# Recurrence gates written into the decay buffer, one more raw weight buffer, and the new instruction order that goes with it

## The chip, the core and the metric

The kernel runs on one core of a Trainium2 chip. The metric is the device time of one execution in microseconds (us). Five engines work side by side, each with its own queue of instructions that it takes strictly in order: PE (TensorE, the matmuls), DVE (VectorE), ACT (ScalarE), POOL (GpSimd) and SP (SyncE, which here issues the loads). An instruction that waits holds up all that stands behind it on its engine.

## The reference: what is computed

A sequence of 256 tokens of width 1024 goes through one recurrent layer (RG-LRU), then keys and values are made once, then comes one attention layer, then a last normalisation. All is fp32. The part that the change touches is the recurrent mixer:

```
h = rmsnorm(x) * (1 + scale(c)) + shift(c)
u, g = split(h @ w_in)
u = causal_conv4(u)
r  = sigmoid(block_diag(u, w_a) + b_a)
gi = sigmoid(block_diag(u, w_x) + b_x)
log_a = -8 * r * softplus(-lam)
a    = exp(log_a)
b_in = sqrt(-expm1(2 * log_a)) * (gi * u)
hs   = scan(a, b_in)                 # h[t] = a[t] * h[t-1] + b_in[t]
x1   = x + gate(c) * ((hs * silu(g)) @ w_out)
```

After it, `x1` is normalised and modulated again (by columns called `colsmk` below), and `k, v = split(h @ w_kv)`; with one block of 256 keys the attention is plain causal attention.

## The kernel before

**Order.** The program records every operation in a `Plan` and then simulates it with a table of costs (`_forward`, `order`). Which ready operation an engine takes next is decided by an urgency per operation, and that urgency is shaken by the list of random seeds `KEEP`. The result is one fixed order for each engine, which is issued as it stands (`issue`). So another seed list, or another set of buffers, gives another order everywhere, though the operations stay the same. All instructions come out of one recorder and carry its line: L434, or L187 for those that the planner may give either to ACT or to DVE (`copy`, `affine`, `scale`). They are told apart by the names of their tiles.

**Weights.** 132 blocks of up to 512 KB come through SP's queue into `NRAW` raw buffers (`rawp`). Each block of a large product is split into a high and a low part (`split_into`: a CAST that makes `..._hi`, then a subtraction on DVE that makes `..._lo`, both 128x1024), and the product is three matmuls (`mm3`). Blocks of the modulation (`g`, `mkh`, `mkc`) feed groups of four small matmuls into `gvg` and `gvmk`, or are summed on DVE and ACT (`maccg`, `macmkh`, `macmkc`) first.

**The recurrent layer.** `conv` makes `uc` on DVE. The rest runs in two halves `j` = 0, 1 of 512 channels, each in two groups of 256 channels. For a group, PE makes `pa` and `px` (block-diagonal products with `uc`); ACT makes the sigmoid of `pa` into `rr`, and `tx`, the tanh form of the second gate, from `px`. For a half, ACT then makes tanh of `rr` into `qg`, exp of `rr` into `ag` (the decays), and a square root of `qg` in place. `ag` and `qg` are the two halves of the tile `aq`. The tables of ACT for sigmoid and tanh, for exp and for the square root differ, so that each switch is an ACT_TABLE_LOAD. DVE then makes `wgx`, runs four scans over `aq`, and multiplies by `sg` (the silu path); `y_hi` (a cast) and `y_lo` (on DVE) follow for each quarter of the channels. The tile `rr` has one buffer, and both halves use it.

**Behind it.** `out_rows("wo")` multiplies by `w_out`: PE takes the four tiles kt 0 to 3 (first half of the channels) for all outputs, 48 matmuls with `r_wo` as target, then some `gvmk` groups, then kt 4 to 7 piece by piece, again 48, then the remaining `gvmk` groups. kt 0, 1 need the first `y_hi`, kt 2, 3 the second, and kt 4 to 7 the third and fourth. `mod_gate("g0")` makes `gsg` from `gvg`; POOL moves it into a row and spreads it over all partitions as `gate_g` (PARTITION_BROADCAST). `resid` then makes each of the four pieces of `x1` (name `x`) with a multiplication by `gate_g` and an addition of `xr` on DVE. `rms` takes four squares (`sq_b`, ACT), two roots (`rv_b`, ACT) and short operations on DVE (`rb_b`, `rn_b`, `ry_b`, `rt_b`), once for each 128 tokens. `norm_T` scales (`xn_b`) and transposes on PE (`tp_b`, eight for each 128 tokens), `x1T` is copied back, `hrmk` applies `colsmk`, `hk_hi` and `hk_lo` are its parts, and the product `v` begins with the first `hk_hi`. From there on PE works through `v`, `k`, `q`, `g`, the attention and `r_wp`.

Of the kernel before, what the change touches and what calls it, by code (L numbers as in the profile page):

```python
# [10 lines left out]
F32 = mybir.dt.float32  # L11
# [3 lines left out]
AF = mybir.ActivationFunctionType  # L15
# [8 lines left out]
NH = 8  # L24
EPS = 1e-6
NEG = -1e30
NRAW = 12
NSPL = 4
NWARM = 20
NWARM2 = 4  # L30
# [9 lines left out]
    g1-1  # L40
"""
KEEP = (
    174134411, 1363847499, 501561012, 479182050, 55063396, 1262196190, 1895791361, 70921978,
    2025245939, 522247948, 1081885112, 902321754, 1806762868, 318745555, 812710329,
    423182004, 2012214809, 1111379318, 858955501, 119445705, 1610912521, 1462030052,
    1370424399,
)

MK_DVE = (2, 3)
# [404 lines left out]
def kernel(ctx: ExitStack, tc: tile.TileContext, x, mod_b, final_norm_g, vecs, pack, out):  # L454
# [5 lines left out]
    V, A, PE, G, SP = (plan.engine(e) for e in ("vector", "scalar", "tensor", "gpsimd", "sync"))  # L460
# [399 lines left out]
    baT = pbT[:, 40:48]  # L860
# [29 lines left out]
    p4 = const.tile([P, KT], F32, name="p4")  # L890
    n8 = const.tile([P, KT], F32, name="n8")
# [34 lines left out]
    for j in range(2):  # L926
# [171 lines left out]
    scale = 1.0 / math.sqrt(P)  # L1098
# [110 lines left out]
```

## Time and profile before

| | |
|---|---|
| median of 3 runs | 255.78 us (255.24 to 255.79) |
| the profiled execution | 255.34 us |
| its span in the trace | 253.6 us, 4919 instructions |
| TensorE clock granted, mean | 0.994 of full speed |
| PE busy | 241.7 us (95%) |
| DVE busy | 210.0 us (83%) |
| ACT busy | 160.0 us (63%) |
| POOL busy | 17.3 us (7%) |
| ACT table loads | 13, 1283 ns each |

The sum of the prediction is made against the profiled execution: 255.34 us, that is a span of 253.6 us and 1.7 us around it. In the timeline views a line gives the start, the length, the engine, the operation with the tile that it writes and those that it reads, and a count where several follow each other; a bracket at the end is the idle time of the engine ahead of it and what ended it.

### The profile page before, as it was taken

The numbers are of one execution on the slowest core, as the hardware profiler recorded it, in microseconds if no ns is written. First come the engines' busy times: TensorE is split into PE (matmuls) and PEld (weight loads), VectorE is DVE, ScalarE is ACT, GpSimd is POOL, SyncE is SP. The second block draws the span as 40 slices with busy tenths as digits, with TensorE's granted clock in tenths as the row PEclk, the third lists the DMA queues.
The fourth block names the chain that finished last, engine by engine and source line by source line (L and its number), as shares of the span: only waits on it lengthen the run. The fifth ranks groups of instructions, "written<-read, shape, count | busy, mean of one in ns | idle before, by whom it ended". The sixth has DMA issues, their size and how long they took to land.

```text
span 253.6 us, 4919 instructions
## 1 busy us (share of the span) xinstructions
PE 241.7 (95%) x1862; PEld 216.0 (85%) x1862; DVE 210.0 (83%) x383; ACT 160.0 (63%) x288; POOL 17.3 (7%) x24
## 2 busy tenths in 40 slices
PE   8899999999999999989999999999999999999980
PEld 8789899998888777857898898999999998879870
DVE  4577399899999999999979998998446999697583
ACT  6675563697599995389834374784438374894252
POOL 4000000000000036200000000010000000023220
PEclk9999999999999999999999999999999999999997
DMA  6999999996599957999999999989965400000003
GB/s 237 410 409 405 408 408 408 410 406 249 149 361 412 378 197 283 405 410 410 406 409 390 400 412 406 406 301 381 388 216 183 169 3 0 1 3 1 1 10 156
DMA packets 20359, 72.24 MB, mean 285 GB/s; under 512 B 2536, under 2 KB 2800, under 8 KB 20336
## 3 DMA queue, kind: packets, MB, share of 16 engines
q1 hardware_dynamic: 19728, 71.20, 72.3%
q0 software_dynamic: 464, 0.54, 0.8%
q8 instruction: 14, 0.23, 0.4%
q10 hardware_dynamic: 144, 0.20, 0.2%
q14 instruction: 9, 0.07, 0.1%
HBM read 70.87 MB, written 1.05 MB: 284 GB/s over the span
## 4 chain that ended last, share of the span: by engine, by line
PE 66%; DVE 19%; ACT 8%; issue 3%; DMA 1%; SPq 0%; DVEq 0%; ACTq 0%
PE g L434 9%; PE v L434 9%; PE u L434 9%; PE r_wp L434 8%; PE pj_wkb L434 5%; PE pj_wqb L434 5%; PE k L434 5%; PE q L434 4%; DVE uc L434 4%; PE ga L434 3%; DVE x L434 3%; PE sc L434 3%; PE oT L434 2%; DVE wo_lo L434 2%; DVE sg L434 2%
## 5 line engine op out<-in xcount | busy, mean ns | idle before, releaser
L434 PE MATMUL g<-h_hi,wgb_lo 128*128 128x256 f32 x64 | 18.0, 282 | 0.0
L434 PE MATMUL g<-h_hi,wgb_hi 128*128 128x256 f32 x64 | 18.0, 281 | 0.0
L434 PE MATMUL g<-h_lo,wgb_hi 128*128 128x256 f32 x64 | 18.0, 281 | 0.0
L434 PE MATMUL u<-h_hi,wu_hi 128*128 128x256 f32 x64 | 17.0, 289 | 0.6 <-ACT h_hi L434 0.6
L434 ACT ACT_TABLE_LOAD x13 | 16.7, 1283 | 0.9 <-PEq L1191 0.7
L434 PE MATMUL u<-h_hi,wu_lo 128*128 128x256 f32 x64 | 17.2, 287 | 0.0
L434 PE MATMUL u<-h_lo,wu_hi 128*128 128x256 f32 x64 | 17.0, 283 | 0.0
L434 DVE SCALAR_TENSOR_TENSOR maccg<-g,csT,maccg 128x1024 f32<-128x1024 f32 x12 | 15.4, 1283 | 0.2
L434 PE MATMUL r_wp<-wp_hi,o_hi 128*128 128x512 f32 (+1 forms) x40 | 14.3, 357 | 0.0
L434 PE MATMUL r_wp<-wp_lo,o_hi 128*128 128x512 f32 (+1 forms) x40 | 14.2, 356 | 0.0
L434 PE MATMUL r_wp<-wp_hi,o_lo 128*128 128x512 f32 (+1 forms) x40 | 14.1, 358 | 0.0
L434 POOL DMA_DIRECT2D row_g<-gsg x8 | 4.2, 532 | 143.2 <-DVE gsg L434 84.8
L434 PE MATMUL v<-wv_hi,hk_hi 128*128 128x512 f32 x32 | 12.4, 397 | 0.6 <-ACT hk_hi L187 0.6
L434 PE MATMUL r_wo<-wo_hi,y_hi 128*128 128x512 f32 x32 | 12.5, 401 | 0.3 <-ACT y_hi L187 0.3
L434 PEld LDWEIGHTS u<-h_hi,wu_hi 128*128 128x128 f32 x64 | 11.4, 189 | 1.6 <-ACT h_hi L434 0.8
L434 DVE TENSOR_TENSOR wgb_lo<-wgb,wgb_hi 128x1024 fp32r<-128x1024 f32 x8 | 9.7, 1218 | 3.7 <-ACT wgb_hi L187 3.7
L434 PE MATMUL v<-wv_lo,hk_hi 128*128 128x512 f32 x32 | 12.6, 395 | 0.0
L434 PE MATMUL r_wo<-wo_lo,y_hi 128*128 128x512 f32 x32 | 12.5, 395 | 0.0
L434 PE MATMUL v<-wv_hi,hk_lo 128*128 128x512 f32 x32 | 12.5, 395 | 0.0
L187 ACT CAST wgb_hi<-wgb 128x1024 fp32r<-128x1024 f32 x8 | 8.4, 1050 | 6.4 <-PE g L434 3.6
L434 PE MATMUL r_wo<-wo_hi,y_lo 128*128 128x512 f32 x32 | 12.1, 394 | 0.0
L434 PEld LDWEIGHTS g<-h_hi,wgb_hi 128*128 128x128 f32 x64 | 12.1, 188 | 0.0
(300 smaller groups left out, 865.4 us busy)
## 6 DMA issues: line engine op xcount, KB each, us to landing
g<-in_pack_dram SPq DMA_DIRECT2D x16, 512.0 KB, 5.9
wu<-in_pack_dram SPq DMA_DIRECT2D x8, 512.0 KB, 10.3
wo<-in_pack_dram SPq DMA_DIRECT2D x8, 512.0 KB, 6.2
mkh<-in_pack_dram SPq DMA_DIRECT2D x8, 512.0 KB, 6.8
mkc<-in_pack_dram SPq DMA_DIRECT2D x8, 512.0 KB, 7.1
wv<-in_pack_dram SPq DMA_DIRECT2D x8, 512.0 KB, 9.9
m1h<-in_pack_dram SPq DMA_DIRECT2D x8, 512.0 KB, 8.6
m1c<-in_pack_dram SPq DMA_DIRECT2D x8, 512.0 KB, 8.5
```

Source lines behind the costliest of these rows:

```text
L187: self.record(eng, fn, args, kw, lambda f=f, args=args, kw=kw: f(*args, **kw))
L434: self.plan.record(self.name, fn, args, kw, lambda: f(*args, **kw))
```

## The change

Three things. The tile `rr` is gone: the sigmoid goes into `ag`, tanh reads `ag`, and exp works in place on `ag`. The 4 KB for each partition that this frees hold a 13th raw buffer. And the seed list is new, 36 seeds in place of 23, so that the whole order is another one.

```diff
-NRAW = 12
+NRAW = 13
...
 KEEP = (
-    174134411, 1363847499, 501561012, 479182050, 55063396, 1262196190, 1895791361, 70921978,
...
+    235379739, 161345772, 1729185277, 1372182491, 1720230322, 837705437, 372798370,
...
         ag, qg = aq[:, 0:4], aq[:, 4:8]
-        rr = tmp.tile([P, 4, S], F32, tag="rr", name=f"rr{j}", bufs=1)
...
-                A.activation(rr[:, 2 * h + m], pr[:, m * S:(m + 1) * S], AF.Sigmoid, bias=baT[:, dd])
+                A.activation(ag[:, 2 * h + m], pr[:, m * S:(m + 1) * S], AF.Sigmoid, bias=baT[:, dd])
...
-            A.activation(qg[:, m], rr[:, m], AF.Tanh, scale=p4[:, dd])
+            A.activation(qg[:, m], ag[:, m], AF.Tanh, scale=p4[:, dd])
...
-            A.activation(ag[:, m], rr[:, m], AF.Exp, scale=n8[:, dd])
+            A.activation(ag[:, m], ag[:, m], AF.Exp, scale=n8[:, dd])
```

The number of matmuls and of table loads stays as it is (1621 and 13), and the orders of POOL and SP are the same; the recorder's lines are L436 and L189 in the new kernel. On PE the products follow each other as before with small exchanges. In the gate products `pa` and `px` now alternate group by group: four matmuls `pa`, four `px`, the next group's four `pa` and four `px`. Of the `gvmk` groups one now stands behind the `gvg` groups ahead of the first `r_wo`, three stand between kt 0, 1 and kt 2, 3 of `r_wo`, and two between kt 2, 3 and kt 4; before, all six stood in that last place. Two groups `gvm` that interrupted `pj_wkb` in two places now stand together. In the other places that count:

ACT before, from the last gates of the second half (`rr_344`, `aq_343`) to its square root; the two `y_hi` are those of kt 0, 1 and kt 2, 3:

```order
L187 CAST y_hi<-sg_323 128x512
L187 CAST wo_1_hi<-wo_1_129 128x1024
L434 ACTIVATE tx_350<-px_349,hbx 128x256
L434 ACTIVATE aq_343<-rr_344,p_301 128x256 x4
L187 CAST y_hi<-sg_323 128x512
L434 ACT_TABLE_LOAD
L434 ACTIVATE aq_343<-rr_344,n_302 128x256 x4
L434 ACTIVATE tg_pj_wgc_351_356<-pj_wgc_351 128x512
L434 ACT_TABLE_LOAD
L434 ACTIVATE aq_343<-aq_343 128x1024
L187 CAST wo_3_hi<-wo_3_135 128x1024
```

ACT now, the same place:

```order
L189 CAST wo_1_hi<-wo_1_129 128x1024
L189 CAST y_hi<-sg_323 128x512
L436 ACTIVATE aq_342<-aq_342,p_301 128x256
L436 ACTIVATE tx_345<-px_344,hbx 128x256
L436 ACTIVATE aq_342<-aq_342,p_301 128x256 x3
L436 ACT_TABLE_LOAD
L436 ACTIVATE aq_342<-aq_342,n_302 128x256 x2
L436 ACTIVATE tg_pj_wgc_349_354<-pj_wgc_349 128x512
L436 ACTIVATE aq_342<-aq_342,n_302 128x256 x2
L436 ACT_TABLE_LOAD
L436 ACTIVATE aq_342<-aq_342 128x1024
L189 CAST y_hi<-sg_323 128x512
```

The second `y_hi` has moved from ahead of the exps of the second half to behind its square root: two table loads, four exps, one tanh and the square root now stand ahead of it. In the first half the square root now comes ahead of the exps, and four casts of `wo` stand between the first half's gates and the first `y_hi`, where two stood.

DVE before, from the first product with `sg` of the second half to the first multiplications of `resid` (`x_357`):

```order
L434 TENSOR_TENSOR sg_323<-aq_343,sg_323 128x512
L434 TENSOR_TENSOR wo_3_lo<-wo_3_135,wo_3_hi 128x1024
L434 SCALAR_TENSOR_TENSOR aq_343<-aq_343,wgx 128x256
L434 TENSOR_TENSOR y_lo<-sg_323,y_hi 128x512
L434 TENSOR_TENSOR sg_323<-aq_343,sg_323 128x512
L434 TENSOR_TENSOR wo_2_lo<-wo_2_136,wo_2_hi 128x1024
L434 TENSOR_TENSOR y_lo<-sg_323,y_hi 128x512
L434 TENSOR_TENSOR wo_3_lo<-wo_3_137,wo_3_hi 128x1024
L434 SCALAR_TENSOR_TENSOR macmkh<-mkh_140,csT,macmkh 128x1024
L434 SCALAR_TENSOR_TENSOR macmkc<-mkc_141,csT,macmkc 128x1024
L434 TENSOR_TENSOR x_357<-r_wo_361,gate_g_377 128x512
L434 TENSOR_TENSOR x_357<-r_wo_362,gate_g_377 128x512
```

DVE now, from the cast of the third `y_hi` to the first multiplication of `resid` (`x_355`):

```order
L189 CAST y_hi<-sg_323 128x512
L436 TENSOR_TENSOR y_lo<-sg_323,y_hi 128x512
L436 TENSOR_TENSOR wo_3_lo<-wo_3_135,wo_3_hi 128x1024
L436 TENSOR_TENSOR wo_2_lo<-wo_2_134,wo_2_hi 128x1024
L436 TENSOR_TENSOR wo_3_lo<-wo_3_137,wo_3_hi 128x1024
L436 SCALAR_TENSOR_TENSOR aq_342<-aq_342,wgx 128x256
L436 TENSOR_TENSOR wo_2_lo<-wo_2_136,wo_2_hi 128x1024
L436 TENSOR_TENSOR sg_323<-aq_342,sg_323 128x512
L436 SCALAR_TENSOR_TENSOR macmkc<-mkc_141,csT,macmkc 128x1024
L436 TENSOR_TENSOR y_lo<-sg_323,y_hi 128x512
L436 SCALAR_TENSOR_TENSOR macmkh<-mkh_140,csT,macmkh 128x1024
L436 TENSOR_TENSOR wv_lo<-wv_146,wv_hi 128x1024
```

Between the second half's multiplication into `wgx` and the first `x` there are now five subtractions of a low part (four `wo`, one `wv`) where three stood, three `y_lo` where two stood, and a cast of `y_hi` that ACT made before. The three `wgx` and scan instructions ahead of the piece shown are the same in both.

DVE before, from the last addition of `resid` to the scaling `xn_b` of the first 128 tokens (the names `ry_b_396` and `ry_b_408` are the first and second 128 tokens):

```order
L434 TENSOR_TENSOR x_357<-x_357,xr 128x512
L434 TENSOR_SCALAR rb_b_403<-ss_b_402,eps 128x1
L434 SCALAR_TENSOR_TENSOR rt_b_397<-ry_b_396,rn_b_395 128x1
L434 TENSOR_SCALAR rb_b_403<-ss_b_402,neps 128x1
L434 SCALAR_TENSOR_TENSOR ry_b_396<-rt_b_397,ry_b_396 128x1
L187 TENSOR_SCALAR xn_b_398<-x_357,ry_b_396 128x1024
```

DVE now, from the same addition to the scaling of the second 128 tokens (`ry_b_394` the first, `ry_b_406` the second 128 tokens):

```order
L436 TENSOR_SCALAR rn_b_393<-ss_b_391,rb_b_389 128x1
L189 CAST wv_hi<-wv_152 128x1024
L436 TENSOR_SCALAR rn_b_405<-ss_b_403,rb_b_401 128x1
L436 RECIPROCAL ry_b_394<-rv_b_392 128x1
L436 SCALAR_TENSOR_TENSOR rt_b_395<-ry_b_394,rn_b_393 128x1
L436 RECIPROCAL ry_b_406<-rv_b_404 128x1
L436 SCALAR_TENSOR_TENSOR rt_b_407<-ry_b_406,rn_b_405 128x1
L436 SCALAR_TENSOR_TENSOR ry_b_394<-rt_b_395,ry_b_394 128x1
L189 TENSOR_SCALAR xn_b_396<-x_355,ry_b_394 128x1024
L436 STREAM_TRANSPOSE gTmk<-gvmk 128x512
L436 SCALAR_TENSOR_TENSOR ry_b_406<-rt_b_407,ry_b_406 128x1
L189 TENSOR_SCALAR xn_b_408<-x_355,ry_b_406 128x1024
```

Before, the first 128 tokens were finished while the last piece of `x` was still being made, and the second `xn_b` was ACT's. Now the chains of both run interleaved behind the last addition, on ACT all four squares stand ahead of both roots, and both `xn_b` are DVE's.

## Rows read from the trace of the kernel before

**Rows 1.** Waits of PE, longest after the start: us in total, times, longest.

```profile
PE tp_b L434 <- ACT x1T L187: 0.8, 1, 0.8
```

**Rows 2.** Timeline of PE, the gate products.

```profile
61.06 0.60 PE L434 MATMUL pa<-uc,gax 128*128 128x256 f32 x2
...
64.54 1.89 PE L434 MATMUL pa<-uc,gax 128*128 128x256 f32 x8
66.27 1.46 PE L434 MATMUL px<-uc,gax 128*128 128x256 f32 x6
```

**Rows 3.** Timeline of ACT, both halves' gates, up to the second half's square root.

```profile
66.47 0.84 ACT L434 ACTIVATE rr<-pa,vT 128x256 f32<-128x256 f32 x2 [3.09 <-PE pa L434]
...
70.66 0.46 ACT L434 ACTIVATE tx<-px,hbx 128x256 f32<-128x256 f32 x1
...
77.82 1.57 ACT L434 ACTIVATE rr<-pa,vT 128x256 f32<-128x256 f32 x4
...
82.74 1.10 ACT L187 CAST wo_hi<-wo 128x1024 fp32r<-128x1024 f32 x1
83.69 0.53 ACT L434 ACTIVATE tx<-px,hbx 128x256 f32<-128x256 f32 x1
...
85.65 0.65 ACT L187 CAST y_hi<-sg 128x512 fp32r<-128x512 f32 x1
86.32 1.28 ACT L434 ACT_TABLE_LOAD   x1
...
92.09 1.03 ACT L187 CAST wo_hi<-wo 128x1024 fp32r<-128x1024 f32 x1
```

**Rows 4.** Timeline of PE, both halves of `r_wo` and the `gvmk` runs.

```profile
82.94 0.50 PE L434 MATMUL r_wo<-wo_hi,y_hi 128*128 128x512 f32 x1 [0.32 <-ACT y_hi L187]
...
94.32 0.64 PE L434 MATMUL gvmk<-mkh,csB 128*32 128x256 f32 x8
...
96.50 0.61 PE L434 MATMUL gvmk<-mkc,csB 128*32 128x256 f32 x8
97.05 0.50 PE L434 MATMUL r_wo<-wo_hi,y_hi 128*128 128x512 f32 x1
...
108.41 0.64 PE L434 MATMUL gvmk<-macmkh,ones 128*32 128x256 f32 x8
```

**Rows 5.** Timeline of DVE, from the second half's `wgx` to the first `xn_b`.

```profile
92.26 1.23 DVE L434 TENSOR_TENSOR wgx<-aq,wgx 128x1024 f32<-128x1024 f32 x1
...
95.29 0.67 DVE L434 TENSOR_TENSOR sg<-aq,sg 128x512 f32<-128x512 f32 x1
95.88 1.22 DVE L434 TENSOR_TENSOR wo_lo<-wo,wo_hi 128x1024 fp32r<-128x1024 f32 x1
97.01 0.69 DVE L434 TENSOR_TENSOR_SCAN aq<-aq,wgx 128x256 f32<-128x256 f32 x1
...
101.67 2.19 DVE L434 SCALAR_TENSOR_TENSOR macmkh<-mkh,csT,macmkh 128x1024 f32<-128x1024 f32 x1
103.78 1.27 DVE L434 SCALAR_TENSOR_TENSOR macmkc<-mkc,csT,macmkc 128x1024 f32<-128x1024 f32 x1
...
107.98 0.20 DVE L434 TENSOR_SCALAR rb_b<-ss_b,eps 128x1 f32<-128x1 f32 x1
...
108.89 0.67 DVE L434 TENSOR_TENSOR x<-r_wo,gate_g 128x512 f32<-128x512 f32 x1
...
110.78 0.75 DVE L187 TENSOR_SCALAR xn_b<-x,ry_b 128x1024 f32<-128x1024 f32 x1
```

**Rows 6.** Timeline of POOL, the two broadcasts of a gate row.

```profile
97.60 5.32 POOL L434 PARTITION_BROADCAST gate_g<-row_g  x1 [6.49 <-issue]
...
230.25 1.29 POOL L434 PARTITION_BROADCAST gate_g<-row_g  x1 [1.25 <-DMA row_g<-gsg]
```

**Rows 7.** Timeline of all engines, from the second `xn_b` to the first `v`.

```profile
112.25 1.15 ACT L187 ACTIVATE xn_b<-x,ry_b 128x1024 f32<-128x1024 f32 x1 [0.83 <-DVE ry_b L434]
...
115.66 0.50 PE L434 MATMUL v<-wv_hi,hk_hi 128*128 128x512 f32 x1 [0.59 <-ACT hk_hi L187]
```

More of the change, by code (lines that the diff above doesn't have):

```diff
@@ L42 @@
 KEEP = (
-    174134411, 1363847499, 501561012, 479182050, 55063396, 1262196190, 1895791361, 70921978,
-    2025245939, 522247948, 1081885112, 902321754, 1806762868, 318745555, 812710329,
-    423182004, 2012214809, 1111379318, 858955501, 119445705, 1610912521, 1462030052,
-    1370424399,
+    235379739, 161345772, 1729185277, 1372182491, 1720230322, 837705437, 372798370,
+    469041122, 805187127, 916564664, 1705839333, 1417637374, 1139869901, 493473457,
+    1043179226, 761050186, 2072417939, 527660131, 619850111, 1896014577, 1153662524,
+    95354911, 1346393068, 839102062, 1294131448, 1979194692, 1929631393, 516464295,
+    2083942596, 959230965, 610772015, 961824923, 1554361591, 2007710663, 1185530256,
+    1355401379,
 )
```

## The prediction, made before the changed kernel was run

> **What bounds the kernel now.** I read the page's first part, then the waits of PE, then the timelines of the engines around those waits. PE is busy for 95% of the span, and from the first products to the last one it runs without a gap except in a few places. The list of its waits is short: the longest after the start is 0.8 us for the second `tp_b` [rows 1], and no entry names a DMA. A change helps here if it shortens one of these waits, and it hurts if it makes a new one. Both ways lead through the stretch from 61 to 116 us, in which one chain runs over three engines: gates on PE [rows 2], ACT's tables and gates [rows 3], `r_wo` on PE [rows 4], scans and `x` on DVE [rows 5], the broadcast on POOL [rows 6], and the first `v` at 115.66, for which PE waits 0.59 [rows 7]. Behind it PE is gapless until the last `r_wp`, so that what moves the first `v` moves the end.
>
> **The buffer alone buys nothing.** The second half's sigmoid starts at 77.82 with no idle time ahead of it [rows 3]: ACT came straight from its table load, so the shared `rr` held nothing up. The 13th raw buffer can only let loads start earlier, and PE never waits for one: I put it at 0, and its bound on either side is 0 as far as the list of waits goes. What is left is the new order, step by step.
>
> **Step 1, gates.** In clean alternation the first half's 16 gate matmuls stand together. The row of eight records from 64.54 to 66.27 is four matmuls, 0.216 a record [rows 2]; 32 records from 61.06 end at 67.98. ACT reacts 0.20 later (66.27 to 66.47), and the two `tx` take 0.39 (1.57 / 4) and 0.46 [rows 3]: the last one ends at 69.03, where before it ended at 70.66 + 0.46 = 71.12. A gain of 2.09 on ACT.
>
> **Step 2, ACT up to the second `y_hi`.** ACT has no idle time from 70.66 to 92.09 [rows 3]. From 71.12 to the end of the second `y_hi`, 85.65 + 0.65 = 86.30, it needed 15.18 before. Now the same stretch holds all of that, and ahead of the second `y_hi` also what stood behind it from 86.32 to 92.09 (two table loads, four exps, a tanh, the square root: 5.77), and a fourth cast of `wo` (83.69 - 82.74 = 0.95). 15.18 + 5.77 + 0.95 = 21.90, so the second `y_hi` ends at 69.03 + 21.90 = 90.93, 4.6 later than before. The first `y_hi` has two casts more ahead of it, 1.90, against the 2.09 gained: it and `r_wo` start at about 82.75 instead of 82.94 [rows 4]. A gain there is nearly all spent.
>
> **Step 3, PE.** 48 matmuls of `r_wo` took 94.32 - 82.94 = 11.38, 24 take 5.69. A `gvmk` group takes (96.50 - 94.32) / 5 = 0.436, and leaving a run 0.55 - 0.436 = 0.11 more [rows 4]; I count as much for entering. PE does kt 0, 1 until 88.44 and three groups until 89.97, and then waits for the second `y_hi` until 90.98: a new wait of 1.0 us, in which everything else of PE is queued behind it. kt 2, 3 and two groups (1.1) bring it to 97.8, where it was at 97.05: 0.7 late. `r_wo` then ends at 108.41 + 0.7 = 109.1, and eight groups later, 3.6, PE is ready for `tp_b` at 112.7.
>
> **Step 4, DVE up to the last multiplication of `resid`.** The square root ends as the second `y_hi` begins on ACT, at 90.28; before, the cast behind it began at 92.09 and `wgx` on DVE at 92.26, 0.17 later [rows 3, 5]. So `wgx` starts at 90.45, 1.8 earlier than before. From there to the last multiplication of `x` took 108.89 - 92.26 = 16.63. Now there are two more subtractions at 1.13 (95.88 to 97.01), one more `y_lo` at 0.59 (95.29 to 95.88) and a cast of `y_hi` at 0.59 with 0.1 until its reader can start; three short operations go behind it, each 0.20 long [rows 5] less 0.09 of overlap with the next (1.22 - 1.13), -0.33. That is +3.21: the last multiplication starts at 90.45 + 16.63 + 3.21 = 110.29, where it was at 108.89. It lies behind PE's part (109.1), so DVE ends last.
>
> This holds 0.92 us that the order alone doesn't explain: `macmkh` took 2.19, `macmkc`, the same operation on the same shape, 1.27 [rows 5]. During `macmkh` POOL's broadcast of `gate_g` ran, which took 5.32 there and 1.29 where it ran alone [rows 6]. So one of the two was in the other's way for about 4 us, and once the other way round. In the new order the broadcast still has to land ahead of the first `x`, DVE is still packed without a gap ahead of it, and both `macmkc` and `macmkh` are still there: I count the 0.92 as paid again, between 0 and 0.92. [...]
>
> **Step 5, from there to the first `v`.** Before, this took 115.66 - 108.89 = 6.77. The first `xn_b` came at 110.78, ahead of the second chain, and the second at 112.25 on ACT [rows 5, 7]. Now the two chains are interleaved behind the last addition, and ACT's first root waits behind the fourth square, so the first `xn_b` comes about when the second did: 112.25 - 110.78 = 1.47 later. Bounds are 0 (the second chain decides both times) and 1.47 (all of it is passed on). PE had waited 0.84 between the two sets of transposes (0.8 in [rows 1]), which now follow each other closely, so I take 1.47 - 0.84 = 0.63. First `v`: 110.29 + 6.77 + 0.63 = 117.69, against 115.66: **+2.03**. In place of the short waits of before stands one for the first `xn_b`, from 112.7 to about 114.4.
>
> **Step 6, behind it.** One interruption less in `pj_wkb` saves what a run costs to leave and to enter, 0.2. In the tail a square of 512 columns moves ahead of other work of ACT; the nearest row for that size is 0.59 on DVE (95.29 to 95.88) [rows 5], so between 0 and -0.6, and I take -0.1, since the last addition there comes only when PE lets it. The other exchanges leave the same work on engines with slack; 0, for nothing of it stands in PE's list of waits.
>
> **Sum.** 255.34 + 2.03 - 0.2 - 0.1 = 257.1. The profiled execution lies 0.44 under the median of the runs shown, which leaves that much doubt on the base.
>
> **Rivals.**
>
> *A, nearly level, 256.2.* The broadcast meets no operation that it can block. DVE's last multiplication is then at 109.37, just behind PE's 109.1, and the time is 257.1 - 0.9 = 256.2. For it: `gsg` is made a little earlier on DVE, so the broadcast may find another neighbour. Against: DVE has no gap there, and the broadcast waited for 4 us before it was let in.
>
> *B, faster, 253.6.* PE stays the only bound: the 2.09 of step 1 carry through, the second `y_hi` comes by 89.97, and DVE's chain, begun 1.8 earlier, hides its additions. Then PE's waits of 0.84, 0.59 and 0.32 go [rows 1, 4, 7], 1.75 in all: 255.34 - 1.75 = 253.6. It decides from the point where ACT needs 1.0 less than step 2 and DVE 3.2 less than step 4, and neither has that much idle time in its rows.
>
> *C, slower still, 258.4.* All of the 1.47 of step 5 is passed on (+0.84), and some of the blocking hits a second operation (up to 0.9, half taken): 257.1 + 1.3.
>
> *D, it doesn't do what it says, 255.3.* The buffer held nothing up, and the new waits of PE are only moved: what PE waits ahead of kt 2, 3 it no longer waits ahead of `tp_b` and `v`. For it: both waits are in one chain. Against: DVE's additions lie between the two.
>
> **How the numbers follow.** Forecast 0.67, A 0.17, B 0.05, C 0.07, D 0.04. A difference of 0.3%, 0.77 us, is about what a measurement of this kernel can tell from none: the level zone is 255.0 to 256.55. Faster is B, 0.05. Level is A, D and 0.02 from the lower edge of the forecast, 0.23. Slower is the rest, 0.72. The range from 255.9 to 258.2 leaves out B, D, the lower edge of A and most of C, together some 0.17.
>
> **What would show it.** Right: a wait of PE of about 1 us for `y_hi` near 90 us, none there before; the second `y_hi` behind the square root, ending near 91; gates on ACT from about 63 and the first half's last `tx` near 69; the last multiplication of `x` near 110; a wait ahead of `tp_b` of 1 to 2 us with DVE's `xn_b` as releaser; the first `v` near 117.7; one of DVE's operations lengthened by 0.9 in 98 to 106 us. Wrong: a first `v` at or ahead of 116, a second `y_hi` ending ahead of 90, or a time that comes from behind 118 us, where I see nothing that changes by more than a few tenths.

## The result, and the profile after

The changed kernel takes 257.88 us (median; 257.56 to 258.99) against 255.70 (255.24 to 255.79) for the kernel before, measured side by side: a ratio of 1.0087, with a 95% interval of 1.0061 to 1.0112. It is slower by 2.2 us. The profiled execution took 258.99, its span is 257.2 us (255.34 and 253.6 before). This is how its page begins: the span, PE's busy time, and the granted clock in 40 slices.

```profile
span 257.2 us, 4921 instructions
...
PE 242.8 (94%) x1862; PEld 216.4 (84%) x1862; DVE 212.1 (82%) x383; ACT 158.8 (62%) x288; POOL 14.3 (6%) x24
...
PEclk9979999999999999999999999999999999999996
```

PE is the busiest engine as before, but the third slice of the clock is a 7. Next, PE's waits in the changed kernel (us in total, times, longest):

```profile
PE u L436 <- ACT h_hi L436: 1.4, 1, 1.4
...
PE r_wo L436 <- ACT y_hi L189: 1.1, 1, 1.1
PE tp_b L436 <- DVE xn_b L189: 1.0, 1, 1.0
PE r_wo L436 <- DVE wo_lo L436: 0.8, 1, 0.8
...
PE v L436 <- DVE hk_hi L189: 0.4, 1, 0.4
PE tp_b L436 <- DVE colsmk L436: 0.4, 1, 0.4
```

The list answers to [rows 1]. The 0.8 for `x1T` is gone from it, three waits of about 1 us have come, and the longest one stands where the prediction has no step: at the first `u`, at 14 us.

To see where the time lies I cut each trace at six starts: the first `u`, the first `pa`, the first `r_wo`, the last multiplication of `x` on DVE (called S), the first `v` and the last `r_wp`. The lengths between them, in us, for all runs that this document tells of ("behind" is the span's end less the start of the last `r_wp`; each ratio is to runs of the kernel before that stood beside it):

| run | median, ratio [interval] | first u | u to pa | pa to r_wo | r_wo to S | S to v | v to last r_wp | behind |
|---|---|---|---|---|---|---|---|---|
| before | 255.70 | 13.74 | 47.32 | 21.88 | 25.95 | 6.77 | 130.15 | 7.79 |
| after | 257.88, 1.0087 [1.0061, 1.0112] | 14.45 | 48.69 | 21.63 | 27.87 | 7.27 | 129.90 | 7.39 |
| x1 | 257.98, 1.0090 [1.0063, 1.0117] | 14.67 | 48.79 | 21.64 | 27.86 | 7.27 | 129.92 | 7.35 |
| x2 | 255.60, 0.9982 [0.9962, 1.0002] | 13.59 | 47.54 | 21.88 | 25.94 | 6.76 | 130.17 | 7.72 |
| x3 | 257.77, 1.0078 [1.0054, 1.0102] | 14.78 | 47.28 | 21.63 | 27.78 | 7.27 | 129.85 | 7.41 |
| x4 | 258.13, 1.0098 [1.0069, 1.0128] | 15.04 | 47.27 | 21.63 | 27.67 | 6.78 | 130.61 | 7.40 |
| x5 | 257.09, 1.0061 [1.0041, 1.0080] | 13.83 | 47.52 | 21.64 | 27.84 | 7.27 | 129.93 | 7.37 |
| x6 | 256.30, 1.0027 [1.0011, 1.0042] | 13.62 | 47.83 | 21.64 | 26.89 | 7.27 | 129.84 | 7.41 |
| x7 | 258.44, 1.0106 [1.0085, 1.0126] | 14.73 | 47.28 | 21.63 | 27.28 | 7.28 | 129.95 | 8.35 |
| x8 | 256.18, 1.0013 [0.9999, 1.0026] | 14.12 | 47.29 | 21.88 | 25.58 | 6.79 | 129.97 | 9.37 |
| x9 | 257.00, 1.0040 [1.0023, 1.0058] | 14.94 | 48.68 | 21.88 | 25.95 | 6.76 | 129.92 | 7.77 |
| x10 | 255.28, 0.9978 [0.9967, 0.9988] | 13.42 | 47.58 | 21.88 | 25.96 | 6.77 | 130.03 | 7.36 |
| x11 | 255.94, 1.0007 [0.9996, 1.0019] | 13.89 | 48.59 | 21.06 | 27.01 | 6.54 | 129.91 | 7.40 |

Read the second line against the first. Of the profiled 3.6 us, 0.71 + 1.37 = 2.08 lie ahead of `pa`, 2.17 between `pa` and `v` (-0.25, +1.92, +0.50), and behind `v` 0.65 comes back (-0.25, -0.40).

**The start.** Three rows of the kernel before, ACT, DVE and PE, ahead of the first `u`:

```profile
12.78 0.90 ACT L434 ACTIVATE h_hi<-tp_a,sg2m 128x128 fp32r<-128x128 f32 x2
12.79 0.90 DVE L434 TENSOR_SCALAR hr_first<-tp_a,sg2m 128x128 f32<-128x128 f32 x2 [0.42 <-ACT sg2m L434]
...
13.74 0.74 PE L434 MATMUL u<-h_hi,wu_hi 128*128 128x256 f32 x4 [0.63 <-ACT h_hi L434]
```

The same work in the changed kernel:

```profile
12.68 0.46 ACT L436 ACTIVATE h_hi<-tp_a,sg2m 128x128 fp32r<-128x128 f32 x1
13.18 0.73 DVE L436 TENSOR_SCALAR hr_first<-tp_a,sg2m 128x128 f32<-128x128 f32 x2 [0.91 <-ACT h_hi L436]
13.94 0.46 ACT L436 ACTIVATE h_hi<-tp_a,sg2m 128x128 fp32r<-128x128 f32 x1 [0.80 <-DVE hr_first L436]
...
14.45 1.22 PE L436 MATMUL u<-h_hi,wu_hi 128*128 128x256 f32 x4 [1.44 <-ACT h_hi L436]
```

Two tiles of PSUM are read here, by ACT for `h_hi` and by DVE for `hr_first`. Before, ACT began with one of them and DVE with the other, and the two engines ran side by side from 12.78. In the new order both begin with the same tile: DVE waits 0.91 for ACT, ACT waits 0.80 for DVE, and PE gets its `h_hi` 0.8 later (it waits 1.44 for 0.63). The section on the change does not name this exchange of the two `hr_first`. Each of the two waits names the other engine's reader as its releaser.

Behind that wait, in this execution, the granted clock fell. The stretches 14 to 16 and 16 to 18 us (us, busy time and instructions of PE, PEld, DVE, ACT and POOL, PEclk, DMA share, GB/s), of before and then of after:

```profile
14.00:16.00 2.00, 2.00 (x40) 1.66 (x40) 1.64 (x3) 1.05 (x1) 0.00 (x0) 1.00 1.02 404
16.00:18.00 2.00, 2.00 (x20) 2.00 (x19) 1.38 (x4) 1.59 (x3) 0.00 (x0) 1.00 1.01 406
```

```profile
14.00:16.00 2.00, 1.55 (x12) 1.31 (x16) 1.56 (x2) 1.10 (x2) 0.00 (x0) 0.55 0.99 391
16.00:18.00 2.00, 2.00 (x36) 1.54 (x27) 0.29 (x1) 1.38 (x2) 0.00 (x0) 0.59 1.03 414
```

Before, the granted clock was 1.00 from 12 to 20 us; in the changed kernel it was 1.00 from 12 to 14, 0.55 and 0.59 in the two stretches shown, and 1.00 again from 18 to 20. From `u` to `pa` it then took 48.69 where it takes 47.28 in three runs with the same wait and no fall (x3, x4, x7): 1.4 us for the fall, in the executions that have it.

**From the gates to S.** In this part all times of after are 2.08 late by the start. ACT, DVE, POOL and PE in order of time:

```profile
70.24 0.84 ACT L436 ACTIVATE tx<-px,hbx 128x256 f32<-128x256 f32 x2
...
92.46 0.60 ACT L189 CAST y_hi<-sg 128x512 fp32r<-128x512 f32 x1
...
92.58 1.23 DVE L436 TENSOR_TENSOR wgx<-aq,wgx 128x1024 f32<-128x1024 f32 x1
93.11 0.50 PE L436 MATMUL r_wo<-wo_hi,y_hi 128*128 128x512 f32 x1 [1.06 <-ACT y_hi L189]
...
98.00 3.50 DVE L436 TENSOR_TENSOR wo_lo<-wo,wo_hi 128x1024 fp32r<-128x1024 f32 x3
100.33 2.33 POOL L436 PARTITION_BROADCAST gate_g<-row_g  x1 [8.64 <-issue]
101.41 1.65 DVE L436 TENSOR_TENSOR_SCAN aq<-aq,wgx 128x256 f32<-128x256 f32 x1
102.98 1.19 DVE L436 TENSOR_TENSOR wo_lo<-wo,wo_hi 128x1024 fp32r<-128x1024 f32 x1
104.23 0.50 PE L436 MATMUL r_wo<-wo_lo,y_hi 128*128 128x512 f32 x1 [0.79 <-DVE wo_lo L436]
...
112.64 0.69 DVE L436 TENSOR_TENSOR x<-r_wo,gate_g 128x512 f32<-128x512 f32 x1
```

The broadcast of [rows 6] is here at 100.33, 2.33 long. The operation that it meets on DVE is no longer `macmkh` (2.19 in [rows 5]; 1.28 now, at 106.50) but the last scan: 1.65, where that of the kernel before took 0.69 [rows 5]. Behind the scan stands a subtraction that makes a `wo_lo`, and PE waits 0.79 for it.

**From S to v.** DVE and PE, the end of the chain:

```profile
116.09 0.75 DVE L189 TENSOR_SCALAR xn_b<-x,ry_b 128x1024 f32<-128x1024 f32 x1
...
116.99 1.06 PE L436 MATMUL tp_b<-ident,xn_b 128*128 128x128 f32 x8 [0.97 <-DVE xn_b L189]
118.44 1.07 PE L436 MATMUL tp_b<-ident,xn_b 128*128 128x128 f32 x8 [0.39 <-DVE colsmk L436]
119.91 0.50 PE L436 MATMUL v<-wv_hi,hk_hi 128*128 128x512 f32 x1 [0.40 <-DVE hk_hi L189]
```

These answer to [rows 7]: one wait for the first `xn_b`, two short ones behind it.

### The profile page after: what moved, and what is told of

The parts are those of the page before. It is cut to its first block, busy times and chain, and to the rows that moved or that the text cites. A ratio compares the mean times of both kernels' runs of the same rounds, so it can differ in the third digit from the quotient of the medians.

```text
span 257.2 us, 4921 instructions
## 1 busy us (share of the span) xinstructions
PE 242.8 (94%) x1862; PEld 216.4 (84%) x1862; DVE 212.1 (82%) x383; ACT 158.8 (62%) x288; POOL 14.3 (6%) x24
## 4 chain that ended last, share of the span: by engine, by line
PE 78%; DVE 8%; ACT 6%; DMA 3%; issue 1%; SPq 1%; DVEq 0%; ACTq 0%
PE u L436 10%; PE g L436 9%; PE v L436 9%; PE r_wp L436 8%; PE pj_wkb L436 5%; PE pj_wqb L436 5%; PE k L436 4%; PE q L436 4%; PE ga L436 4%; PE pj_wgc L436 3%; PE r_wo L436 3%; DMA wu<-in_pack_dram 3%; DVE x L436 3%; PE px L436 3%; PE pa L436 3%; PE sc L436 3%
## 5 line engine op out<-in xcount | busy, mean ns | idle before, releaser
L436 PE MATMUL u<-h_hi,wu_hi 128*128 128x256 f32 x64 | 17.1, 300 | 1.4 <-ACT h_hi L436 1.4
L436 PE MATMUL g<-h_hi,wgb_hi 128*128 128x256 f32 x64 | 18.0, 282 | 0.0
L436 PE MATMUL g<-h_lo,wgb_hi 128*128 128x256 f32 x64 | 18.0, 282 | 0.0
L436 PE MATMUL g<-h_hi,wgb_lo 128*128 128x256 f32 x64 | 18.0, 282 | 0.0
L436 PE MATMUL u<-h_lo,wu_hi 128*128 128x256 f32 x64 | 17.2, 287 | 0.0
L436 PE MATMUL u<-h_hi,wu_lo 128*128 128x256 f32 x64 | 16.7, 283 | 0.0
L436 DVE SCALAR_TENSOR_TENSOR maccg<-g,csT,maccg 128x1024 f32<-128x1024 f32 x12 | 15.4, 1283 | 0.2
L189 ACT CAST wgb_hi<-wgb 128x1024 fp32r<-128x1024 f32 x8 | 8.4, 1051 | 10.0 <-PE q L436 4.9
L436 PE MATMUL r_wp<-wp_hi,o_hi 128*128 128x512 f32 (+1 forms) x40 | 14.3, 357 | 0.0
L436 PE MATMUL r_wp<-wp_lo,o_hi 128*128 128x512 f32 (+1 forms) x40 | 14.2, 358 | 0.0
L436 PE MATMUL r_wp<-wp_hi,o_lo 128*128 128x512 f32 (+1 forms) x40 | 14.0, 351 | 0.0
L436 PEld LDWEIGHTS u<-h_hi,wu_hi 128*128 128x128 f32 x64 | 11.7, 198 | 2.6 <-ACT h_hi L436 1.6
L436 PE MATMUL r_wo<-wo_hi,y_hi 128*128 128x512 f32 x32 | 12.5, 406 | 1.2 <-ACT y_hi L189 1.1
L436 PE MATMUL r_wo<-wo_lo,y_hi 128*128 128x512 f32 x32 | 12.7, 397 | 0.8 <-DVE wo_lo L436 0.8
L436 PE MATMUL v<-wv_hi,hk_hi 128*128 128x512 f32 x32 | 12.6, 398 | 0.4 <-DVE hk_hi L189 0.4
L436 DVE TENSOR_TENSOR wgb_lo<-wgb,wgb_hi 128x1024 fp32r<-128x1024 f32 x8 | 9.8, 1224 | 3.5 <-ACT wgb_hi L189 3.4
L436 PE MATMUL v<-wv_lo,hk_hi 128*128 128x512 f32 x32 | 12.6, 395 | 0.0
L436 PE MATMUL v<-wv_hi,hk_lo 128*128 128x512 f32 x32 | 12.6, 395 | 0.0
L189 ACT CAST wv_hi<-wv 128x1024 fp32r<-128x1024 f32 x7 | 7.3, 1048 | 8.2 <-PE r_wo L436 3.8
L436 POOL DMA_DIRECT2D row_g<-gsg x8 | 4.2, 533 | 144.3 <-DVE gsg L436 85.4
L436 PEld LDWEIGHTS g<-h_hi,wgb_lo 128*128 128x128 f32 x64 | 12.1, 188 | 0.0
```

Source lines behind the costliest of these rows:

```text
L189: self.record(eng, fn, args, kw, lambda f=f, args=args, kw=kw: f(*args, **kw))
L436: self.plan.record(self.name, fn, args, kw, lambda: f(*args, **kw))
```

## The experiments

The theory with which I went in: only the new order counts, the buffers nothing; of the loss, one part is the start, one the longer chain on DVE, one the interleaved normalisation. The rivals stand with each run. In the diffs by rows, a row that is moved stands with - where the changed kernel (or the kernel named) has it and with + where the experiment has it.

**x1, the changed kernel once more, and x2, the changed code in the order of before.** x1 has no edit. x2 keeps the gates in `aq`, two `wo` buffers and 13 raw ones, and takes every engine's rows from the kernel before:

```diff
-        best = self._forward(urge)
...
+        best = self._forward(urge, {e: [int(i) for i in l.split()] for e, l in TAKE.items()})
```

> The changed kernel as it is, for a second profile. In its first profile the first product u began at 14.45 us behind a wait of 1.44 us for h_hi (0.63 before), and the granted clock was 0.55 and 0.59 in the four microseconds behind it; that execution took 258.99, the other three 257.56 to 258.17. Theory (the loss lies in the stretch from the gates to the first v, the slow start belongs to single executions): 257.6, 1.9 above the kernel before, and in a profile without the slow start the first gate product pa near 61, the first v near 117.8. Rival (the new order also makes the start slower): pa near 63 again and the clock low behind the first u again.

> The changed code (gates written into the decay buffer, 13 raw buffers) with the order of every engine taken from the kernel before, instruction by instruction. Theory (only the order costs): 255.7, within 0.3 of the kernel before, the second half's sigmoid again directly behind its table load, the first v at 115.7. Rival (the buffers cost or gain themselves: the exp in place, the 13th block in flight): slower by more than 0.8 or faster by more than 0.8.

x1 measured 257.98, with the fallen clock in its profile too (0.75, 0.50 and 0.89 in the three stretches from 14 to 20 us); of its six executions the two with the lowest mean clock took 259.0 and 259.3, the others 257.5 to 258.2. So x1's rival holds: the late start is no matter of a single execution. x2 measured 255.60, its interval holds 1, and all its lengths are those of before within 0.25. So the buffers show neither a cost nor a gain (0.4% at the most); the loss lies in the order.

**x3, the second `y_hi` early.** On ACT the second `y_hi`, on DVE its `y_lo`, each directly behind the first, as in the kernel before; everything else as changed.

```diff
 CAST wo_1_hi<-wo_1_129 128x1024
-CAST y_hi<-sg_323 128x512
+CAST y_hi<-sg_323 128x512 x2
 ACTIVATE aq_342<-aq_342,p_301 128x256
...
 ACTIVATE aq_342<-aq_342 128x1024
-CAST y_hi<-sg_323 128x512
 CAST wo_3_hi<-wo_3_135 128x1024
```

> The changed kernel with one thing moved: the second y_hi on ACT and the second y_lo on DVE go directly behind the first ones, ahead of the tanh and exp of the second half. Theory (DVE's chain to the last piece of x ends last, the new wait of PE ahead of kt 2, 3 is covered): the wait of 1.06 ahead of kt 2, 3 goes, a wait of about 0.9 appears ahead of kt 4, and the time stays within 0.3 of the changed kernel; the chain on ACT and DVE is as long as it was. Rival (the wait of PE is the loss): 1.0 faster than the changed kernel, that is about 256.6, and the first v 1.0 earlier.

The wait ahead of kt 2, 3 is gone, and PE waits longer for DVE's `wo_lo`, in two places:

```profile
99.24 0.51 PE L456 MATMUL r_wo<-wo_lo,y_hi 128*128 128x512 f32 x1 [0.35 <-DVE wo_lo L456]
...
103.06 0.50 PE L456 MATMUL r_wo<-wo_lo,y_hi 128*128 128x512 f32 x1 [1.22 <-DVE wo_lo L456]
```

0.35 + 1.22 = 1.57, against 0.79 in the changed kernel; from `pa` to `v` it takes 56.68 against 56.77. A wait of 1 us taken away brings 0.1. The last multiplication of `x` came hardly earlier (`r_wo` to S 27.78 for 27.87): DVE's chain ends last here, and PE waits for it at one place or at the other.

**x4, the normalisation in the order of before.** ACT's and DVE's rows from the pieces of `x` to the first columns of `v`, the second `xn_b` on ACT again. The piece on ACT:

```diff
+ACTIVATE sq_b_387,ss_b_388<-x_355 128x512
+ACTIVATE sq_b_390,ss_b_391<-x_355 128x512
+ACTIVATE rv_b_392<-ss_b_391,rb_b_389 128x1
+ACTIVATE sq_b_399,ss_b_400<-x_355 128x512
 CAST wv_hi<-wv_149 128x1024
-ACTIVATE sq_b_387,ss_b_388<-x_355 128x512
-ACTIVATE sq_b_399,ss_b_400<-x_355 128x512
-ACTIVATE sq_b_390,ss_b_391<-x_355 128x512
 ACTIVATE sq_b_402,ss_b_403<-x_355 128x512
-ACTIVATE rv_b_392<-ss_b_391,rb_b_389 128x1
```

> The changed kernel with ACT and DVE in the order of the kernel before from the pieces of x to the first columns of v (squares, roots, xn_b, x1T, hrmk, hk_hi, hk_lo, wv parts), the second xn_b on ACT again. Theory (step 5 of the prediction, 0.5 to 0.6 of the loss, and the rest lies ahead of it): 0.5 to 0.7 faster than the changed kernel, the first v more than 1 us earlier and some of it lost again in waits inside v. Rival (the interleaving is hidden by the wait for the last piece of x): within 0.2. Rival (all of 1.47 was passed on): 1.3 or more faster.

From S to `v` it takes 6.78, the 6.77 of before: the 0.5 of this part does come from these rows. But the time did not fall (258.13), because from `v` to the last `r_wp` it takes 130.61 instead of 129.90. PE's rows, 4 us into `v`:

```profile
121.50 0.40 PE L460 MATMUL v<-wv_hi,hk_hi 128*128 128x512 f32 x1
122.21 0.51 PE L460 MATMUL v<-wv_lo,hk_hi 128*128 128x512 f32 x1 [0.31 <-DVE wv_lo L460]
```

The second begins 0.71 behind the first, where 0.23 is usual: 0.48 of the 0.71 that this part is longer is lost at this one place; for the rest no wait shows. An earlier `v` that then waits for its weights' low part is no gain: the moved rows put DVE's `wv_lo` later. The 0.5 is real as a length and was worth nothing as it was tried.

**x5, the two `hr_first` exchanged.** One exchange on DVE in the changed kernel, back to the tile order of before:

```diff
+TENSOR_SCALAR hr_first<-tp_a_244,sg2m_250 128x128
 TENSOR_SCALAR hr_first<-tp_a_236,sg2m_250 128x128
-TENSOR_SCALAR hr_first<-tp_a_244,sg2m_250 128x128
 TENSOR_TENSOR h_lo<-hr_first,h_hi 128x256
```

> The changed kernel with two instructions exchanged: on DVE the first hr_first reads the second tile tp_a and the second one the first, as in the kernel before, so that DVE and ACT (h_hi) read different PSUM tiles at the same time. Everything else as in the changed kernel. Theory (the slow start is this order: DVE waited 0.91 for ACT's h_hi and ACT's second h_hi then 0.80 for DVE, so that PE's wait ahead of u was 1.44 instead of 0.63): the wait ahead of u is 0.6 again, the first pa comes near 61.1 instead of 62.1, the clock stays high behind u in every profile, the time is 0.8 to 1.1 under the changed kernel, 256.6 to 256.9, and no execution lies over 258. Rival (the late start comes with the data, not with the order): the wait stays at 1.4 and the time at 257.7.

```profile
13.83 0.74 PE L451 MATMUL u<-h_hi,wu_hi 128*128 128x256 f32 x4 [0.63 <-ACT h_hi L451]
```

The wait is 0.63 again, the clock 1.00 from 10 to 22 us, and the median 257.09: 0.8 under the changed kernel, 0.9 under x1, and a little over the 256.6 to 256.9 expected. One of the six executions took 258.11, where none was expected over 258; its mean clock, 0.996, is the highest of the six. Everything behind `pa` is unchanged to 0.03.

**x9, the reverse: the kernel before with that one exchange.**

```diff
+TENSOR_SCALAR hr_first<-tp_a_236,sg2m_250 128x128
 TENSOR_SCALAR hr_first<-tp_a_244,sg2m_250 128x128
-TENSOR_SCALAR hr_first<-tp_a_236,sg2m_250 128x128
```

> The kernel before with one exchange on DVE: of its two hr_first instructions (12.79, 0.90 for both) the one that reads the tile that ACT's first h_hi reads too now stands first, as in the changed kernel; nothing else is moved. Theory (the start is a cause of its own): DVE's and ACT's instructions on one tile go one behind the other, PE's wait ahead of u is about 1.4 instead of 0.63, the first u comes at 14.5 instead of 13.74, and the median rises by 0.8 to 1.0, to 256.5 to 256.7; in executions in which the granted clock falls behind that wait, to 0.55 to 0.75 at 14 to 18 us as in the profiles of the changed kernel, by 2 or more. Rival (the start of the changed kernel is late because of other rows that the new order moves, and the exchange alone is covered): the wait stays near 0.63 and the time within 0.3 of the kernel before, 255.4 to 256.0.

First PE's row, then the two stretches of the clock as above:

```profile
14.94 1.23 PE L449 MATMUL u<-h_hi,wu_hi 128*128 128x256 f32 x4 [1.45 <-ACT h_hi L449]
```

```profile
14.00:16.00 2.00, 1.06 (x4) 0.93 (x4) 1.48 (x4) 1.39 (x2) 0.00 (x0) 0.67 1.02 399
16.00:18.00 2.00, 2.00 (x34) 1.43 (x33) 0.48 (x1) 1.04 (x1) 0.00 (x0) 0.50 1.02 408
```

257.00 against 255.88 beside it, over the 256.5 to 256.7 expected, and the lengths behind `pa` are those of before within 0.23. Two rows in the other order, with nothing else changed, cost 1.1 us of the median, and in the profiled execution the clock fell behind their wait. The start is a cause of its own.

That the wait must bring the fall does not follow. The same stretch in x3, whose wait at `u` is 1.4 as well:

```profile
14.00:16.00 2.00, 1.22 (x24) 1.08 (x28) 1.48 (x3) 1.40 (x2) 0.00 (x0) 1.00 1.03 401
```

What decides between executions stays open. Nor is a low mean clock found behind the longer wait alone: one of 17 executions of the kernel before (258.52, beside x1 to x4) and two of the twelve of x6 (257.51 and 257.33) had 0.987, as one of the two longest of x1 had. They were not profiled, so where their clock was low is not known.

**x6, x5 with DVE's and ACT's rows between the gates and `x` in the order of before.** On DVE, in part:

```diff
+TENSOR_TENSOR y_lo<-sg_323,y_hi 128x512
 CAST wo_2_hi<-wo_2_134 128x1024
 SCALAR_TENSOR_TENSOR wgx<-aq_342,wgx 128x1024
+TENSOR_TENSOR wo_2_lo<-wo_2_134,wo_2_hi 128x1024
 SCALAR_TENSOR_TENSOR sg_323<-tg_pj_wgc_349_354,pj_wgc_349 128x512
-CAST wo_2_hi<-wo_2_136 128x1024
 TENSOR_TENSOR wgx<-aq_342,wgx 128x1024
-TENSOR_TENSOR y_lo<-sg_323,y_hi 128x512
...
-CAST y_hi<-sg_323 128x512
```

> The kernel with the two instructions exchanged, and on ACT and DVE the operations between the gates and the pieces of x (second tanh and exp, y_hi, y_lo, the scans, the wo and macmk operations, the first two wv_hi) in the order of the kernel before; PE, the first half's gates and the normalisation as in the changed kernel. Theory (step 4, the additions on DVE's chain, is the larger part of what is left): 0.8 to 1.0 under the kernel with the exchange alone, so 255.7 to 256.0; the wait ahead of kt 2, 3 gone, the last piece of x about 1 us earlier. Rival (the loss of the stretch is in the normalisation and in PE's new runs): less than 0.3 gained.

256.30: 0.79 less than x5, at the lower edge of what was expected, and the length from `r_wo` to S is 0.95 shorter. So the rows of step 4 are shown as a cause. It is not back at 25.95: 0.94 remain. The rows of POOL and DVE show that the broadcast has found another neighbour, and PE waits 0.65 for a `y_hi`.

```profile
100.47 1.52 POOL L465 PARTITION_BROADCAST gate_g<-row_g  x1 [9.96 <-issue]
100.74 2.19 DVE L465 TENSOR_TENSOR wo_lo<-wo,wo_hi 128x1024 fp32r<-128x1024 f32 x1
```

```profile
97.81 1.19 PE L465 MATMUL r_wo<-wo_hi,y_hi 128*128 128x512 f32 x4 [0.65 <-ACT y_hi L209]
```

The DVE row is the subtraction that takes 1.22 elsewhere; now it takes 2.19.

**x7 and x8, the changed kernel and the kernel before without the first broadcast.** In both, the gate of the first layer is a constant:

```diff
-        G.partition_broadcast(gb, row)
+        if l:
+            G.partition_broadcast(gb, row)
+        else:
+            G.memset(gb, 0.0)
```

> The changed kernel without POOL's first broadcast: gate_g of the first layer is set to zero by a memset in its place, so that the recurrent layer's product does not reach x; every other instruction and every order is as in the changed kernel. Theory (the broadcast and two-input operations of DVE block each other): the scan at 101 us takes 0.6 instead of 1.65, PE's wait of 0.8 for wo_lo goes or shrinks, the first v comes 0.5 to 0.9 earlier and the time is 0.5 to 0.9 under the changed kernel. Rival (the scan is long for another reason, or the time is passed on to another wait): the time stays within 0.2.

> The kernel before without POOL's first broadcast, by the same memset; the recurrent layer's product does not reach x. Theory: macmkh takes 1.3 instead of 2.19, and the first v comes 0.5 to 0.9 earlier (255.0 to 255.3). Rival (PE's part of the stretch ends as late as DVE's, so that the 0.9 was covered): within 0.2 of the kernel before.

The lengthened operation is short again in both. The scan in x7, and `macmkh` and the last multiplication of `x` in x8:

```profile
100.67 0.68 DVE L449 TENSOR_TENSOR_SCAN aq<-aq,wgx 128x256 f32<-128x256 f32 x1
```

```profile
102.01 1.28 DVE L447 SCALAR_TENSOR_TENSOR macmkh<-mkh,csT,macmkh 128x1024 f32<-128x1024 f32 x1
...
108.87 0.69 DVE L447 TENSOR_TENSOR x<-r_wo,gate_g 128x512 f32<-128x512 f32 x1 [0.47 <-PE r_wo L447]
```

DVE gets 0.97 back in x7 and 0.91 in x8. At `v` (counted from `pa`) 0.58 of it arrives in x7 (56.77 to 56.19) and 0.35 in x8 (54.60 to 54.25), where DVE then waits 0.47 for PE. So the blocking costs the changed kernel 0.6, the kernel before 0.35, and the difference between the two is 0.2. `macmkh`, the scan and x6's `wo_lo` subtraction were each 0.9 to 1.0 longer where a broadcast ran: 2.19 for 1.28, 1.65 for 0.68 and 2.19 for 1.22. Why these were hit, no view shows.

The whole times of these two runs (258.44 and 256.18, where 0.5 to 0.9 less than without the edit was expected) can't be used for that price. In both the part behind the last `r_wp` grew, by 1.0 and 1.6. In x8 the broadcast that is left begins at 234.62, where [rows 6] have it at 230.25. The kernel before first, then x8 (POOL and DVE):

```profile
239.32 1.30 POOL L434 TENSOR_TENSOR ot<-x,fgB 128x512 f32<-128x512 f32 x1 [7.77 <-DVE x L434]
```

```profile
234.62 1.31 POOL L447 PARTITION_BROADCAST gate_g<-row_g  x1 [6.23 <-DVE wp_lo L447]
...
243.10 2.54 POOL L447 TENSOR_TENSOR ot<-x,fgB 128x512 f32<-128x512 f32 x2 [7.17 <-PE r_wp L447]
...
244.32 1.86 DVE L447 TENSOR_TENSOR x<-x,x 128x512 f32<-128x512 f32 x1
```

In [rows 6] POOL stands idle for 6.49 ahead of the first broadcast and for 1.25 ahead of the second. In x8, where the second is the only one, 6.23 stand ahead of it, so the pause went here with the execution's first broadcast; what POOL does in it no view shows. The first of POOL's two products stood at 239.32 before; now a pause of 7.17 stands ahead of both, and they run at 243.10, beside an addition of `x` on DVE that takes 1.86 instead of 0.68.

**x10, the order of before up to the first `v`, that of the changed kernel behind it.** The edit is that of x2 with another list of rows.

> The changed code (recurrence gates, two wo buffers, 13 raw ones), with every engine's instructions in the order of the kernel before up to those of the first v, and in the changed kernel's order behind it. Theory (the new order costs only ahead of v, and its part behind v is shorter by itself): as far as v like the kernel before (u at 13.6 to 13.8, v near 115.7), from v to the last r_wp 129.9 instead of 130.15, the tail behind it 7.4 instead of 7.79, so 0.65 under the kernel before: 254.9 to 255.2. Rival (what is shorter behind v in the changed kernel comes of its being late there, since transfers and casts then have more time): v to the last r_wp 130.1 or more, the tail 7.7, and 255.5 to 255.8, level with the kernel before.

255.28, 0.6 under the kernel before beside it (254.9 to 255.2 was expected), and the interval (0.9967 to 0.9988) leaves 1 out. It is the fastest kernel of this study. The part behind the last `r_wp` is 7.36, from `v` to there 130.03: 0.43 of the gain is the tail, 0.12 the rest. The new order's tail is better by itself, and the rival (that it only looks shorter because it starts late) falls for the tail; for the stretch ahead of it the new order shows no gain: here it takes 130.03, and x8 and x9, with PE's order of before, take 129.97 and 129.92, as little as the changed kernel. What makes the 0.25 there is open.

**x11, x10 with more rows moved ahead of `v`.** On ACT, in part, against x10:

```diff
 CAST wo_3_hi<-wo_3_135 128x1024
+ACTIVATE macmkc<-mkc_143,csT 128x1024
 CAST wo_2_hi<-wo_2_136 128x1024
+CAST y_hi<-sg_323 128x512
 CAST wo_3_hi<-wo_3_137 128x1024
-CAST y_hi<-sg_323 128x512 x2
 ACTIVATE macmkh<-mkh_142,csT 128x1024
-ACTIVATE macmkc<-mkc_143,csT 128x1024
+CAST y_hi<-sg_323 128x512
```

> As the run with the old order up to v, with further rows of ACT and DVE moved by some places ahead of v: at the start, among the casts and gates, and between the second y_hi and v, so that what PE waits for stands ahead of what it doesn't wait for (the second y_hi of each pair between two casts, macmkc ahead of macmkh, xn's statistics without a weight cast among them). Theory (PE's waits ahead of v, of which the kernel before has 0.63 at u, about 1 at the second transposed x and some 0.9 at v, come of rows that stand too early): each becomes 0.1 to 0.3 shorter, v at about 115.0, 0.7 under the run with the old order up to v: 254.2 to 254.6. Rival (these waits are set by the length of the chain, or each place that is freed is taken by another wait): v within 0.2 of 115.7 and the time within 0.2 of that run.

It failed: 255.94, 0.66 over x10. The waits at `u`, `tp_b` and `v` did become shorter, by 0.1 to 0.3 each, but two new ones came. PE and ACT, in order of time:

```profile
19.11 0.74 PE L546 MATMUL u<-h_hi,wu_hi 128*128 128x256 f32 x4 [0.38 <-ACT h_hi L298]
...
96.40 1.15 ACT L298 ACTIVATE macmkc<-mkc,csT 128x1024 f32<-128x1024 f32 x1 [2.29 <-DMA mkc<-in_pack_dram]
...
99.06 0.50 PE L546 MATMUL r_wo<-wo_hi,y_hi 128*128 128x512 f32 x1 [1.16 <-ACT y_hi L298]
```

The larger one is made by the row that was moved: `macmkc` on ACT, put ahead of the second half's first `y_hi`, stands 2.29 us for its weight block, which is not there yet, and the `y_hi` behind it comes 1.16 late for PE. From `pa` to `v` this run takes 54.61, just as x10 does, so that what the shorter waits gave there went into the 1.16; the profile is 1.0 longer between `u` and `pa`, where the 0.38 stands. The rival's mechanism is the right one, each place that was freed was taken by another wait, but its size is not: the time was to stay within 0.2.

## Why the prediction was right, and where it was not

The time, 257.88, lies in the range, 0.8 above the forecast of 257.1; the direction is right. That it lies in the range is in part luck: a cause of 0.8 to 1.1 us for which nothing was forecast took up the upper part of it, and the profiled execution (258.99), in which the clock fell, lies outside. It is nearer to rival C's 258.4 than to the forecast, though C's mechanism is not what the rows show (0.50 of the 1.47 was passed on, and one operation was lengthened). The step that is wrong is the first one, the choice of the stretch: "Both ways lead through the stretch from 61 to 116 us". I read the waits "after the start" and left the start itself out, though PE's wait of 0.63 for `h_hi` stands in that list, and though the two exchanged rows stand in the order ahead of it. The prediction named "a time that comes from behind 118 us" as what would make it wrong; it came from ahead of 16. x5 and x9 price it, one in either direction, at 0.8 to 1.1 us of the median; where the clock falls it is 0.8 for the wait and 1.4 to 1.5 for the fall. Without it (x5) the median is 257.09. That this is the forecast to 0.01 is luck too: the sum started from an execution 0.4 under the median, and its steps came to less than their 1.73 (below).

From `pa` on, the steps can be compared one by one; times of after are given less the 2.08.

| step | predicted | measured |
|---|---|---|
| 1: first half's last `tx` ends on ACT | 69.03 | 70.24 + 0.84 - 2.08 = 69.00 |
| 2: second `y_hi` ends | 90.93 | 92.46 + 0.60 - 2.08 = 90.98 |
| 2: first `r_wo` | 82.75 | 84.77 - 2.08 = 82.69 |
| 3: PE's new wait ahead of kt 2, 3 | 1.0 | 1.06 |
| 4: second `wgx` starts | 90.45 | 92.58 - 2.08 = 90.50 |
| 4: S | 110.29 | 112.64 - 2.08 = 110.56 |
| 4: blocking by the broadcast | 0.92 | 0.97 |
| 5: S to `v`, more than before | 0.63 | 0.50 |
| first `v`, more than before | 2.03 | 119.91 - 2.08 - 115.66 = 2.17 |
| 6: behind `v` | -0.2 - 0.1 | -0.25 - 0.40 |

*Steps 1 to 3* are right as sums of rows. Step 3 told a wait of 1.0 us, and x3 shows what the sum had taken for granted: this wait decides nothing as long as DVE's part ends behind PE's. Taking it away gave 0.1.

*Step 4* is right to 0.3 (S 1.67 later than before, 1.40 in the sum): x6 gives 0.95 back by putting the rows back, the rest is open. Its size holds the blocking, and that was right for another operation than I named. I had written "`macmkc` and `macmkh` are still there"; it was a scan that was hit, with PE waiting behind it for `wo_lo`. Three orders gave three different victims (`macmkh`, the scan, a `wo_lo`) and nearly one price at the operation, 0.91 to 0.97. In x11 it is a fourth, a `y_lo`, by 0.6:

```profile
98.62 1.30 POOL L546 PARTITION_BROADCAST gate_g<-row_g  x1 [8.16 <-issue]
...
99.03 1.29 DVE L546 TENSOR_TENSOR y_lo<-sg,y_hi 128x512 fp32r<-128x512 f32 x1 [0.41 <-ACT y_hi L298]
```

This subtraction takes 0.69 elsewhere, and it ends 0.4 behind the broadcast. Of this price 0.6 reaches `v` in the changed kernel and 0.35 before it (x7, x8), so counting it as paid again was right to 0.2. Rival A needed a broadcast that lengthens no operation of DVE, and in none of the orders looked at here did it find that place.

*Step 5* is right in its place: x4 shows that the interleaved rows make the 0.5. What it didn't say is that the rows also decide when DVE makes `wv_lo`, so that putting them back as they were, alone, gave nothing.

*Step 6* was sized too small in the tail, 0.40 instead of 0.1, within the bound that it named. x10 shows it without a late start: 0.43 of that kernel's 0.6 lie there. Its 0.2 for `pj_wkb` looks right beside 0.25, but the order is not shown to make it: x8 and x9 are as short there in the order of before.

*The buffers* at 0: x2 measures 0.9982 [0.9962, 1.0002], so they cost nothing that can be measured, and bring 0.4% at the most.

In sum: 2.17 - 0.25 - 0.40 = 1.52 for the stretches of the prediction, where its steps were to give 1.73, and 2.08 for the start in the profiled execution, for which nothing was forecast.

**Open.** Why the granted clock falls in some executions behind the 1.4 us wait and not in others, from the same rows. What shortens the stretch behind `v` by 0.25 in the changed kernel, and in x8 and x9 too. And 0.94 us that x6 still has between `r_wo` and S over the kernel before: the blocked `wo_lo` and PE's wait of 0.65 for a `y_hi` stand there, but no run takes them apart.

## What to carry to other kernels

When a change reshuffles an order, read every wait of the critical engine, those of the first microseconds too, and look at what stands in the new order right ahead of each: one exchange of two short rows cost nearly as much here (0.8 to 1.1 us) as the whole stretch that the prediction had worked out step by step (1.3, x5). A new wait of the bound engine was no loss here where another chain ended behind it (x3); look for that chain before you price a wait. And a gain in one stretch counts only when the next stretch takes it: compare the lengths between fixed points of the trace, not the length of the waits.

## What the runs showed of the hardware that was not expected

- Readers on ACT and DVE of one PSUM tile went one behind the other, 0.46 of ACT at 12.68 and then DVE from 13.18 (0.73 for its two tiles); with the tiles taken in opposite order both ran at once, 0.90 each from 12.78. That is 0.8 us at `u` for 128x128 pieces.
- After one wait of 1.44 us at 13 us the granted clock was 0.55 and 0.59 in the next two stretches of 2 us (after), 0.67 and 0.50 (x9), 0.75 and 0.50 (x1), and 1.00 in three other runs with the same wait. The fall cost 1.4 to 1.5 us between `u` and `pa`.
- The length of the broadcast says little of what it costs: 5.32 with `macmkh` at 2.19 [rows 5, 6], 2.33 with a scan at 1.65, 1.52 with a `wo_lo` at 2.19. The price on DVE was 0.9 to 1.0 in these three, and 0.6 in x11, where the broadcast took 1.30.
- POOL's long pause stood ahead of the first broadcast of the execution: 6.49 and then 1.25 in the kernel before [rows 6], 6.23 in x8, where only the later one is left. That one began 4.4 us later for it (234.62 for 230.25), and the span behind the last `r_wp` grew by 1.6.
